# Hybrid mLSTM and HGRN2 decoder layer on one core: denominators summed on VectorE, the last norm's sums in halves and its variance earlier

## The chip, the cores and the metric

One core of a Trainium2 chip. The metric is device time in microseconds of one launch. The weights come from HBM, everything else stays on the chip between the stages except for some intermediate tiles that are spilled to HBM and loaded back. Engines: TensorE (PE, with its weight loads as PEld), VectorE (DVE), ScalarE (ACT), GpSimd (POOL) and SyncE (SP), which issues nearly all DMAs; POOL issues eight near the end.

## The reference

One step of a decoder layer for 256 prompt tokens and 64 sample tokens (8 sequences of 8), 320 tokens in all, all in 4-byte floats. Cut to what the change touches:

```python
# mLSTM, per head (4 heads, DK 256, DV 512), chunkwise
s   = einsum('bhtk,bhsk->bhts', qc, kc) * d
num = einsum('bhts,bhsv->bhtv', s, vc) + w_inter * einsum('bhtk,bhkv->bhtv', qc, C)
den = sum(s, axis=-1) + w_inter * einsum('bhtk,bhk->bht', qc, n)
h   = num / maximum(abs(den), exp(-m_t))
# layer
x1  = LayerNorm(alpha * x + mix, ln1_g, ln1_b)
hid = square(relu(x1 @ w_up))
y   = LayerNorm(alpha * x1 + hid @ w_down, ln2_g, ln2_b)
```

Beside y the outputs are the final mLSTM and HGRN2 states of both groups (for the prompt: Cp, 4 heads of 256 x 512, and Sp, 8 heads of 128 x 256).

## The kernel before

Activations lie transposed, a tile being 128 features by 320 tokens. All dense layers are one stream of 304 weight tiles of 2048 x 128, in the order of a table: the gates and the input projections of the mLSTM heads (stage up to 400 us), those of the HGRN2 heads, the two branch projections, the output projection, and four groups of 16 up and 16 down tiles. A 4-byte product is made of fast products on halves: a number is split into a high half (a copy on ScalarE, `ACT wh`, or `bb`) and a low half (a subtraction on VectorE, line 491), and three products xh.wh, xl.wh and xh.wl are added in PSUM. A tile is two units of 1024 rows; a unit is 8 x 3 = 24 products. A unit's weights land in one of three raw buffers (`wr`) and are split into a pair of buffers from the list `hl_free`: three pairs `wh`, `wl` from the start, and five wide ones in `bb` in the late stages, of which one (`wx[4]`) holds halves for the first norm and is then given back to the list.

Beside this stream run chains: small generators of the form "acquire a buffer, wait for an event, issue one instruction on this engine". A planner written in Python (`Sched`) keeps a clock for each engine, and after each triple of wide products lets every chain issue what its clock says is ready. The order that results is fixed in the program; on the chip each engine takes its own list in order and waits on semaphores. `Pool` objects hand out buffers, PSUM banks among them (`mbank`, `sbank`).

The change touches these chains:

- `m_S` (one per mLSTM head) makes the gated score blocks in E: columns 0 to 127 for the first half of the prompt against itself, 128 to 255 and 256 to 383 for the second half against both halves, 384 to 511 (partitions 64 to 127) for the sample.
- `m_num` makes the numerators of the prompt and its denominators, as products of a block of E with a column of ones: one for the first half, two that are added in PSUM for the second.
- `m_sample` does the same for the sample: one product for the block of E, two for the halves of `qn`, which holds query times normaliser.
- `m_C` and `h_S` make the prompt's final states behind the last weights, with operands that were spilled to HBM and come back by POOL's DMAs into buffers that the weights leave free. `m_C` makes two products of six parts per head into `oC`, `h_S` one per head into `oS`.
- `ln_add`, `ln_sum`, `ln_pre`, `ln_final`, `ln_scale` are the two norms. The sums S1 (of z) and S2 (of z squared) are added up over tiles on VectorE, and the sum over partitions is a product with a matrix of ones: in `total` on halves, elsewhere on 4-byte numbers. After four tiles a first mean `cb` is taken out of z. Tile 15 is not added but goes into PSUM by products of its own (`ln_final`), on top of `ln_pre`. `ln_scale` makes mean M, variance X and the reciprocal root RS.
- `y` subtracts the mean from the 16 tiles of z (line 1960), multiplies by the root (line 1965); `yb_` applies scale and shift on ScalarE and stores two tiles by one DMA.

Of the kernel before, what the change touches and what calls it, by code (L numbers as in the profile page):

```python
# [256 lines left out]
def post(ev):  # L257
    return ("set", ev)
# [51 lines left out]
class Program:  # L310
# [48 lines left out]
    def carve(self):  # L359
# [30 lines left out]
        self.qz = Pool([self.qz0])  # L390
        self.tst = Pool([B(320) for _ in range(2)])
        self.tst2 = B(320)
# [24 lines left out]
        self.sg = Pool([Part(self.f2, 4912)(320), self.tst2])  # L417
        B = Part(self.f2, 4304)
        self.sr = Pool([B(320) for _ in range(2)])
# [493 lines left out]
    def m_S(self, h):  # L913
# [22 lines left out]
        yield ("dve", dve(128), lambda: v.tensor_tensor(ss[64:128, 128:256], E[64:128, 384:512], f(ss[64:128, 0:128]), ALU.subtract))  # L936
        yield ("act", act(256), lambda: self.A(ss[0:64], f(ss[64:128])))
        yield post(m["S"])

# [119 lines left out]
    def m_num(self, h):  # L1059
# [12 lines left out]
        yield ("pe", 212, lambda: self.mm(db[:, 0:1], E[:, 0:128], one, start=True, stop=True))  # L1072
        yield ("pe", 212, lambda: self.mm(db[:, 1:2], E[:, 128:256], one, start=True, stop=False))
        yield ("pe", 212, lambda: self.mm(db[:, 1:2], E[:, 256:384], one, start=False, stop=True))
        for i in range(2):
# [29 lines left out]
    def m_C(self, h):  # L1105
        k = yield acq(self.kx)
        kt = yield ("pool", 1000, lambda: self.nc.gpsimd.dma_start(
            k.rearrange("p x s k -> p (x s k)").rearrange("p (y k) -> p y k", k=128), self.kD[h].rearrange("y p k -> p y k")))
        w = yield acq(self.vx)
        vt = yield ("pool", 1000, lambda: self.nc.gpsimd.dma_start(w, self.vD[h]))  # L1110
        e = Ev()
        e.t = max(kt, vt) + 4000.0
        yield wait(e, self.main_end)
        for c in range(2):
            if h:
                yield wait(self.ln[1]["fin"])
            b = yield acq(self.mbank)
            yield ("pe", 6 * pe_r(512), lambda: [self.mm(
                b, k.rearrange("p x s k -> p (x s k)")[:, 512 * x + 256 * c + 128 * s:512 * x + 256 * c + 128 * s + 128], w[:, y, s, :], start=n == 0, stop=n == 5)
                for n, (s, x, y) in enumerate((s, x, y) for s in range(2) for x, y in ((0, 0), (0, 1), (1, 0)))])  # L1120
            if c == 1:
                yield post(self.mh[h]["C"])
            if h < 2 and c == 0:
                yield ("dve", dve(512, True), lambda: self.nc.vector.tensor_copy(self.oC[h][:, c, :], b))
            else:
                yield ("act", act(512, True), lambda: self.A(self.oC[h][:, c, :], b))
            yield rel(self.mbank, b)
            yield ("sp", 620, lambda: self.dma(self.d["Cp"][h, :, c, :], self.oC[h][:, c, :]))
        yield rel(self.vx, w)

    def place(self, to, x):
# [13 lines left out]
    def m_sample(self, h):  # L1145
# [8 lines left out]
        for c in range(2):  # L1154
            qc = cap(qz, 256 * c, [[136, 2], [32, 4], [1, 8]])
            yield ("dve", dve(64), lambda: v.tensor_tensor(qc, by_token(qk[:, c, :], 256, False), by_token(bc, 640, False), ALU.mult))
            n4 = cap(self.n0[:, h, c, :], 0, [[4, 2], [1, 4], [0, 8]])
            yield ("dve", dve(64), lambda: v.tensor_tensor(by_token(qn, 128 * c, True), qc, n4, ALU.mult))
        yield post(m["QW"])
        nb = yield acq(self.sbank)  # L1160
# [420 lines left out]
    def h_S(self, h):  # L1581
# [7 lines left out]
        yield ("pe", 2 * pe_f(256), lambda: [self.mm(  # L1589
            b[:, 0:256], x[:, 128 * i:128 * i + 128], x[:, 256 + 256 * i:512 + 256 * i], start=i == 0, stop=i == 1) for i in range(2)])  # L1590
        if h < 4:
            yield ("act", act(256, True), lambda: self.A(self.oS[:, h, :], b[:, 0:256]))
# [151 lines left out]
    def ln_add(self, n, j, z, pre):  # L1744
# [4 lines left out]
        if j < 4:  # L1749
# [39 lines left out]

    def total(self, p, x, hl):  # L1790
        hi, lo = hl[:, 0, :], hl[:, 1, :]
        yield from self.split(x, hi, lo)
        for i, y in enumerate((hi, lo)):
            yield ("pe", 147, lambda: self.mm(p[:, :TOK], self.ones.bitcast(F32R), y, start=i == 0, stop=i == 1))

# [33 lines left out]
    def ln_scale(self, n):  # L1829
# [9 lines left out]
        for p in st["p"]:  # L1839
            yield rel(self.sbank, p)  # L1840
        yield ("dve", dve(TOK, mode=2), lambda: v.tensor_scalar(X, X, 0.0, EPS, ALU.max, ALU.add))
        yield ("act", act(TOK), lambda: self.A(RS, X, AF.Ln))
        yield ("act", act(TOK), lambda: self.A(RS, RS, AF.Exp, scale=-0.5))
# [108 lines left out]
    def y(self):  # L1952
# [3 lines left out]
        yield wait(st["m"])  # L1956
        for i in range(KT + 6):
            if i < KT:
                z = self.acc[:, i, :]
                yield ("dve", dve(TOK), lambda: v.tensor_tensor(z, z, self.lnb[3], ALU.subtract), (0.0,))  # L1960
            if i == 5:
                yield wait(st["end"])
            if i > 5:
                z = self.acc[:, i - 6, :]
                t = yield ("dve", dve(TOK), lambda: v.tensor_tensor(z, z, self.lnb[4], ALU.mult), (0.0,))
                self.s.spawn(self.yb_(i - 6, z), 0, t)

# [8 lines left out]
    def run(self, pool):  # L1976
# [12 lines left out]
        self.vD = [self.dr.tile([128, 2, 2, 512], F32, name=f"vD{j}") for j in range(MH)]  # L1989
        self.ln = [dict(c=Ev(), end=Ev(), pre=Ev(), m=Ev(), fin=Ev(), s=[Ev() for _ in range(KT)]) for _ in range(2)]  # L1990
        self.xq, self.xq_ev = [None] * KT, [Ev() for _ in range(KT)]
# [82 lines left out]
```

## Time and profile before

| | |
|---|---|
| three runs | 2311.4, 2311.3, 2310.22 us, median 2311.3 |
| profiled execution | 2310.56 us, of which 2308.7 us span |
| granted TensorE clock | 0.999 |
| HBM traffic | 183 GB/s over the span |
| first state product behind the stream starts | 2281.72 us |
| last state product ends | 2300.8 us |

Times inside the span count from its first instruction. In the timeline a row is: start, duration, engine, line, operation, output tile <- input tiles, shapes, count, and in brackets the idle time before it and who ended it. Line 346 is the helper of every ScalarE operation and line 352 that of every product, so tiles tell them apart: `misc` is the column of ones, `ones` the matrix of ones, `f` a work area of VectorE, `f3m` the tiles of z, `vec` scale and shift, `oC` and `oS` the final states. A 4-byte product shows as two records (x2).

### The profile page before, as it was taken

The numbers are of one execution on the slowest core, as the hardware profiler recorded it, in microseconds if no ns is written. First come the engines' busy times: TensorE is split into PE (matmuls) and PEld (weight loads), VectorE is DVE, ScalarE is ACT, GpSimd is POOL, SyncE is SP. The second block draws the span as 40 slices with busy tenths as digits, with TensorE's granted clock in tenths as the row PEclk, the third lists the DMA queues.
The fourth block names the chain that finished last, engine by engine and source line by source line (L and its number), as shares of the span: only waits on it lengthen the run. The fifth ranks groups of instructions, "written<-read, shape, count | busy, mean of one in ns | idle before, by whom it ended". The sixth has DMA issues, their size and how long they took to land.

```text
span 2308.7 us, 38882 instructions
## 1 busy us (share of the span) xinstructions
PE 2299.2 (100%) x15712; PEld 2258.4 (98%) x15712; DVE 1365.3 (59%) x2333; ACT 1040.1 (45%) x1664; POOL 13.3 (1%) x37
## 2 busy tenths in 40 slices
PE   9999999999999999999999999999999999999998
PEld 9999999999999999999999999999999999999997
DVE  6566667666767776555555767654444444444455
ACT  5443444555556565444433446533433343234333
POOL 0000000000000000000000000000000000000000
PEclk9999999999999999999999999999999999999999
DMA  7677797666556565555555654444444444444466
GB/s 282 209 248 250 236 292 240 204 189 187 183 182 200 170 191 171 176 172 177 170 175 174 213 165 156 146 147 149 152 148 154 146 152 150 148 154 146 154 214 190
DMA packets 214573, 424.94 MB, mean 184 GB/s; under 512 B 83572, under 2 KB 110068, under 8 KB 213368
## 3 DMA queue, kind: packets, MB, share of 16 engines
q1 hardware_dynamic: 209512, 415.97, 55.7%
q0 software_dynamic: 4736, 6.29, 1.1%
q8 instruction: 123, 2.02, 0.4%
q14 instruction: 58, 0.48, 0.1%
q10 hardware_dynamic: 144, 0.20, 0.0%
HBM read 371.48 MB, written 50.90 MB: 183 GB/s over the span
## 4 chain that ended last, share of the span: by engine, by line
PE 99%; ACT 1%; DVE 0%; issue 0%; ACTq 0%; POOL 0%; DVEq 0%; POOLq 0%
PE bank L352 98%; ACT f3m L346 0%; PE bank L954 0%; PE bank L1465 0%; DVE f3m L1960 0%; ACT f L346 0%; PE bank L1470 0%; PE bank L1519 0%; PE bank L1022 0%; PE bank L1626 0%; PE bank L1191 0%; ACT oC L346 0%; ACT oS L346 0%; ACT bb L346 0%; ACT xh L346 0%
## 5 line engine op out<-in xcount | busy, mean ns | idle before, releaser
L352 PE MATMUL bank<-xh,wh 128*128 128x320 f32 (+1 forms) x2432 | 781.3, 322 | 0.0
L352 PE MATMUL bank<-xh,wl 128*128 128x320 f32 (+1 forms) x2432 | 752.2, 310 | 0.0
L352 PE MATMUL bank<-xl,wh 128*128 128x320 f32 (+1 forms) x2432 | 750.0, 309 | 0.0
L491 DVE TENSOR_TENSOR wl<-wr,wh 128x1024 fp32r<-128x1024 f32 x426 | 522.1, 1226 | 381.4 <-ACT wh L346 378.5
L346 ACT ACTIVATE wh<-wr 128x1024 fp32r<-128x1024 f32 x426 | 450.9, 1059 | 514.9 <-PE bank L352 498.1
L352 PEld LDWEIGHTS bank<-xh,wh 128*128 128x128 f32 x2432 | 458.1, 189 | 18.0 <-issue 15.5
L352 PEld LDWEIGHTS bank<-xl,wh 128*128 128x128 f32 x2432 | 458.4, 189 | 3.3
L352 PEld LDWEIGHTS bank<-xh,wl 128*128 128x128 f32 x2432 | 458.0, 188 | 0.2 <-DVE wl L491 0.2
L491 DVE TENSOR_TENSOR bb<-wr,bb 128x1024 fp32r<-128x1024 f32 x176 | 215.7, 1225 | 227.6 <-ACT bb L346 227.5
L346 ACT ACTIVATE bb<-wr 128x1024 fp32r<-128x1024 f32 x176 | 186.4, 1059 | 311.4 <-PE bank L352 293.9
L352 PE MATMUL bank<-xh,bb 128*128 128x320 f32 (+1 forms) x1280 | 285.4, 309 | 0.0
L352 PE MATMUL bank<-rxb,bb 128*128 128x320 f32 x1208 | 276.3, 309 | 0.0
L352 PE MATMUL bank<-ra,wh 128*128 128x320 f32 x988 | 265.9, 309 | 0.0
L352 PE MATMUL bank<-ra,bb 128*128 128x320 f32 x1096 | 264.3, 309 | 0.7 <-DVE ra L1657 0.7
L352 PEld LDWEIGHTS bank<-xh,bb 128*128 128x128 f32 x1280 | 215.0, 188 | 0.0
L352 PEld LDWEIGHTS bank<-rxb,bb 128*128 128x128 f32 x1208 | 204.2, 188 | 0.2
L352 PE MATMUL bank<-xl,bb 128*128 128x320 f32 (+1 forms) x640 | 197.7, 309 | 0.0
L352 PEld LDWEIGHTS bank<-ra,bb 128*128 128x128 f32 x1096 | 187.1, 188 | 1.2 <-DVE ra L1657 0.9
L352 PEld LDWEIGHTS bank<-ra,wh 128*128 128x128 f32 x988 | 176.3, 188 | 0.0
L352 PE MATMUL bank<-rxb,wh 128*128 128x320 f32 x548 | 169.0, 308 | 0.0
L352 PE MATMUL bank<-rxb,wl 128*128 128x320 f32 x548 | 169.0, 308 | 0.0
L352 PEld LDWEIGHTS bank<-xl,bb 128*128 128x128 f32 x640 | 120.4, 188 | 0.2 <-DVE xl L1885 0.2
(262 smaller groups left out, 2195.3 us busy)
## 6 DMA issues: line engine op xcount, KB each, us to landing
wr<-wt SPq DMA_DIRECT2D x602, 512.0 KB, 3.4
rx<-C SPq DMA_DIRECT2D x34, 256.0 KB, 4.8
Cs<-rx SPq DMA_DIRECT2D x34, 256.0 KB, 5.3
f<-C SPq DMA_DIRECT2D x30, 256.0 KB, 5.2
Cs<-f SPq DMA_DIRECT2D x30, 256.0 KB, 5.0
f<-first SPq DMA_DIRECT2D x6, 704.0 KB, 10.3
vD<-ra SPq DMA_DIRECT2D x4, 1024.0 KB, 5.6
f<-S SPq DMA_DIRECT2D x8, 512.0 KB, 6.3
```

The costliest lines, as they stand in the source:

```text
L346: return self.nc.scalar.activation(out, in_, func, **kw)
L352: self.nc.tensor.matmul(*a, **kw)
L491: self.V().tensor_tensor(lo, raw, hi.bitcast(F32), ALU.subtract)
```

## The change

Denominators: in `m_S` VectorE adds the second half's two blocks, and `m_num` has one product for them; in `m_sample` VectorE adds the two halves of `qn`, and later the block of E onto it, and one product is left. Last norm: its three sums over partitions that were products on 4-byte numbers (`ones` with S1 after four tiles, S1 and S2 in `ln_pre`) are made by `total` on halves, as in the first norm; the halves lie in `wx[4]`, which is therefore no longer given back. In `y` one subtraction instead of six is issued ahead of the variance, two more wait for it, and the others alternate with the multiplications. The evictions of `m_C` and `h_S` become chains of their own, all of `m_C`'s on ScalarE, and all but the first product of `m_C` wait until the last norm's sums are issued. Two work areas move by 128 columns.

```diff
@@ m_S
         yield ("act", act(256), lambda: self.A(ss[0:64], f(ss[64:128])))
+        yield ("dve", dve(128), lambda: v.tensor_tensor(E[:, 256:384], E[:, 256:384], E[:, 128:256], ALU.add))
         yield post(m["S"])
@@ m_num
-        yield ("pe", 212, lambda: self.mm(db[:, 1:2], E[:, 128:256], one, start=True, stop=False))
-        yield ("pe", 212, lambda: self.mm(db[:, 1:2], E[:, 256:384], one, start=False, stop=True))
+        yield ("pe", 212, lambda: self.mm(db[:, 1:2], E[:, 256:384], one, start=True, stop=True))
@@ m_C
-            if h:
+            if h or c:
                 yield wait(self.ln[1]["fin"])
...
-            if h < 2 and c == 0:
-                yield ("dve", dve(512, True), lambda: self.nc.vector.tensor_copy(self.oC[h][:, c, :], b))
-            else:
-                yield ("act", act(512, True), lambda: self.A(self.oC[h][:, c, :], b))
...
+            self.s.spawn(self.C_out(h, c, b), 0, self.s.t["pe"])
@@ m_sample
+        yield ("dve", dve(128), lambda: v.tensor_tensor(qn[:, 0:128], qn[:, 0:128], qn[:, 128:256], ALU.add))
         yield post(m["QW"])
...
+        yield ("dve", dve(128), lambda: v.tensor_tensor(qn[64:128, 0:128], qn[64:128, 0:128], E[64:128, 384:512], ALU.add))
         db = yield acq(self.sbank)
-        yield ("pe", 212, lambda: self.mm(db[:, 0:1], E[:, 384:512], self.one, start=True, stop=False))
-        for c in range(2):
-            yield ("pe", 212, lambda: self.mm(db[:, 0:1], qn[:, 128 * c:128 * c + 128], self.one, start=False, stop=c == 1))
+        yield ("pe", 212, lambda: self.mm(db[:, 0:1], qn[:, 0:128], self.one, start=True, stop=True))
@@ ln_add
-                if n == 0:
-                    yield from self.total(p, S1, self.lns[0])
-                else:
-                    yield ("pe", pe_f(TOK), lambda: self.mm(p[:, :TOK], self.ones, S1, start=True, stop=True))
+                yield from self.total(p, S1, self.lns[0])
...
-            self.hl_free.append((self.s.t["pe"], self.wx[4]))
@@ ln_pre
-            yield ("pe", pe_f(TOK), lambda: self.mm(p[i][:, :TOK], self.ones, self.lnb[i], start=True, stop=False))
+            yield from self.total(p[i], self.lnb[i], self.lns[1 + i], False)
@@ ln_scale
         yield ("dve", dve(TOK, mode=2), lambda: v.tensor_scalar(X, X, 0.0, EPS, ALU.max, ALU.add))
+        if n:
+            yield post(st["x"])
@@ y
-        for i in range(KT + 6):
+        for i in range(KT + 3):
...
-            if i == 5:
+            if i == 0:
+                yield wait(st["x"])
+            elif i == 2:
                 yield wait(st["end"])
-            if i > 5:
+            if i > 2:
```

Three places show how the planner's order moves. First TensorE, at the last sample denominators of the first mLSTM head, where `misc` is the column of ones, `f_76` the area of E and `qn`, `ra` the operands of other small products, and `xh`, `wh` the wide stream. Before:

```order
L352 MATMUL bank_85<-misc,f_76 128x1
L352 MATMUL bank_82<-xh,wh 128x320
L352 MATMUL bank_82<-xl,wh 128x320
L352 MATMUL bank_82<-xh,wl 128x320
L352 MATMUL bank_88<-ra 128x512
L352 MATMUL bank_82<-xh,wh 128x320
L352 MATMUL bank_82<-xl,wh 128x320
L352 MATMUL bank_82<-xh,wl 128x320
L352 MATMUL bank_85<-misc,f_76 128x1
```

Now, the same place:

```order
L352 MATMUL bank_88<-ra 128x512
L352 MATMUL bank_85<-misc,f_76 128x1
L352 MATMUL bank_82<-xh,wh 128x320
L352 MATMUL bank_82<-xl,wh 128x320
L352 MATMUL bank_82<-xh,wl 128x320
L352 MATMUL bank_88<-ra 128x512
```

One denominator product is left of three, and it stands right behind another small product, with no wide one between.

Second VectorE, from the eviction of the last tile (bank_81) on; line 1960 (now 1963) subtracts the mean, 1838 (now 1839) makes the variance, 1844 to 1846 (now 1847 to 1849) the root, 1965 (now 1970) multiplies. Before:

```order
L1940 TENSOR_TENSOR f3m<-f3m,bank_81 128x320
L1124 COPY oC<-bank_85 128x512
L1960 TENSOR_TENSOR f3m<-f3m,f_76 128x320 x6
L1838 SCALAR_TENSOR_TENSOR f_76<-bank_84,f_76 128x320
L1841 TENSOR_SCALAR f_76<-f_76 128x320
L1844 SCALAR_TENSOR_TENSOR f_76<-f_76 128x320
L1124 COPY oC<-bank_88 128x512
L1845 TENSOR_TENSOR f_76<-f_76 128x320
L1846 SCALAR_TENSOR_TENSOR f_76<-f_76 128x320
L1960 TENSOR_TENSOR f3m<-f3m,f_76 128x320
L1965 TENSOR_TENSOR f3m<-f3m,f_76 128x320
```

Now:

```order
L1943 TENSOR_TENSOR f3m<-f3m,bank_81 128x320
L1963 TENSOR_TENSOR f3m<-f3m,f_76 128x320
L1839 SCALAR_TENSOR_TENSOR f_76<-bank_84,f_76 128x320
L1842 TENSOR_SCALAR f_76<-f_76 128x320
L1963 TENSOR_TENSOR f3m<-f3m,f_76 128x320 x2
L1847 SCALAR_TENSOR_TENSOR f_76<-f_76 128x320
L1848 TENSOR_TENSOR f_76<-f_76 128x320
L1849 SCALAR_TENSOR_TENSOR f_76<-f_76 128x320
L1963 TENSOR_TENSOR f3m<-f3m,f_76 128x320
L1970 TENSOR_TENSOR f3m<-f3m,f_76 128x320
```

The variance moves ahead of all but one subtraction, and both copies of state blocks are gone from VectorE.

Third ScalarE, from the eviction of the mean and its square on (`f_76<-bank_87`, now `f_76<-bank_86`; `f_76<-f_76` are logarithm and exponential of the root; `f3m<-f3m,vec` is scale and shift of a tile of y). Before:

```order
L346 ACTIVATE f_76<-bank_87 128x320 x2
L346 ACTIVATE oC<-bank_86 128x512
L346 ACTIVATE f_76<-f_76 128x320 x2
L346 ACTIVATE oC<-bank_82 128x512
L346 ACTIVATE oC<-bank_83 128x512
L346 ACTIVATE f3m<-f3m,vec 128x320 x2
L346 ACTIVATE oC<-bank_81 128x512
L346 ACTIVATE f3m<-f3m,vec 128x320 x2
L346 ACTIVATE oC<-bank_85 128x512
L346 ACTIVATE f3m<-f3m,vec 128x320 x2
L346 ACTIVATE oC<-bank_86 128x512
```

Now:

```order
L346 ACTIVATE oC<-bank_87 128x512
L346 ACTIVATE f_76<-bank_86 128x320 x2
L346 ACTIVATE f_76<-f_76 128x320
L346 ACTIVATE oC<-bank_85 128x512
L346 ACTIVATE f_76<-f_76 128x320
L346 ACTIVATE oC<-bank_88 128x512
L346 ACTIVATE oC<-bank_82 128x512
L346 ACTIVATE f3m<-f3m,vec 128x320
L346 ACTIVATE oC<-bank_81 128x512
L346 ACTIVATE f3m<-f3m,vec 128x320 x2
L346 ACTIVATE oC<-bank_87 128x512
L346 ACTIVATE f3m<-f3m,vec 128x320 x2
```

The eviction of the first state product now stands ahead of the mean, that of the second has moved from ahead of the logarithm to between it and the exponential, and one scaled tile, no longer two, stands ahead of the next eviction.

More of the change, by code (lines that the diff above doesn't have):

```diff
@@ L390, in carve @@
         self.qz = Pool([self.qz0])
-        self.tst = Pool([B(320) for _ in range(2)])
+        self.tst = Pool([B(256) for _ in range(2)])
         self.tst2 = B(320)
@@ L417, in carve @@
         self.sg = Pool([Part(self.f2, 4912)(320), self.tst2])
-        B = Part(self.f2, 4304)
+        B = Part(self.f2, 4176)
         self.sr = Pool([B(320) for _ in range(2)])
@@ L1122, in m_C, with C_out @@
                 yield post(self.mh[h]["C"])
-            if h < 2 and c == 0:
-                yield ("dve", dve(512, True), lambda: self.nc.vector.tensor_copy(self.oC[h][:, c, :], b))
-            else:
-                yield ("act", act(512, True), lambda: self.A(self.oC[h][:, c, :], b))
-            yield rel(self.mbank, b)
-            yield ("sp", 620, lambda: self.dma(self.d["Cp"][h, :, c, :], self.oC[h][:, c, :]))
+            self.s.spawn(self.C_out(h, c, b), 0, self.s.t["pe"])
         yield rel(self.vx, w)
+    def C_out(self, h, c, b):
+        yield ("act", act(512, True), lambda: self.A(self.oC[h][:, c, :], b))
+        yield rel(self.mbank, b)
+        yield ("sp", 620, lambda: self.dma(self.d["Cp"][h, :, c, :], self.oC[h][:, c, :]))
     def place(self, to, x):
@@ L1590, in h_S, with S_out @@
             b[:, 0:256], x[:, 128 * i:128 * i + 128], x[:, 256 + 256 * i:512 + 256 * i], start=i == 0, stop=i == 1) for i in range(2)])
+        self.s.spawn(self.S_out(h, b), 0, self.s.t["pe"])
+    def S_out(self, h, b):
         if h < 4:
@@ L1788, in ln_add, with total @@
             self.s.spawn(self.ln_pre(n), 0)
-    def total(self, p, x, hl):
+    def total(self, p, x, hl, stop=True):
         hi, lo = hl[:, 0, :], hl[:, 1, :]
@@ L1793, in total @@
         for i, y in enumerate((hi, lo)):
-            yield ("pe", 147, lambda: self.mm(p[:, :TOK], self.ones.bitcast(F32R), y, start=i == 0, stop=i == 1))
+            yield ("pe", 147, lambda: self.mm(p[:, :TOK], self.ones.bitcast(F32R), y, start=i == 0, stop=stop and i == 1))
     def ln_sum(self, j, z):
@@ L1960, in y @@
                 yield ("dve", dve(TOK), lambda: v.tensor_tensor(z, z, self.lnb[3], ALU.subtract), (0.0,))
-            if i == 5:
+            if i == 0:
+                yield wait(st["x"])
+            elif i == 2:
                 yield wait(st["end"])
-            if i > 5:
-                z = self.acc[:, i - 6, :]
+            if i > 2:
+                z = self.acc[:, i - 3, :]
                 t = yield ("dve", dve(TOK), lambda: v.tensor_tensor(z, z, self.lnb[4], ALU.mult), (0.0,))
-                self.s.spawn(self.yb_(i - 6, z), 0, t)
+                self.s.spawn(self.yb_(i - 3, z), 0, t)
     def yb_(self, j, z):
@@ L1989, in run @@
         self.vD = [self.dr.tile([128, 2, 2, 512], F32, name=f"vD{j}") for j in range(MH)]
-        self.ln = [dict(c=Ev(), end=Ev(), pre=Ev(), m=Ev(), fin=Ev(), s=[Ev() for _ in range(KT)]) for _ in range(2)]
+        self.ln = [dict(c=Ev(), end=Ev(), pre=Ev(), m=Ev(), fin=Ev(), x=Ev(), s=[Ev() for _ in range(KT)]) for _ in range(2)]
         self.xq, self.xq_ev = [None] * KT, [Ev() for _ in range(KT)]
```

## The prediction

> **What bounds the kernel now.** I read the page first, then the table of waits of TensorE, then windows, then the timeline at the places that the change touches.
>
> From the page, busy time by engine and the granted clock in 40 slices:
>
> ```profile
> PE 2299.2 (100%) x15712; PEld 2258.4 (98%) x15712; DVE 1365.3 (59%) x2333; ACT 1040.1 (45%) x1664; POOL 13.3 (1%) x37
> PEclk9999999999999999999999999999999999999999
> ```
>
> The waits of TensorE over the whole span (waited for: total us, times, longest):
>
> ```profile
> PE bank L352 <- POOL ones L634: 1.0, 1, 1.0
> PE bank L352 <- DVE ra L1657: 0.7, 1, 0.7
> ```
>
> TensorE runs without a gap at full clock; 1.7 us is all that it waits for another engine. Up to its last product the time is the sum of what is issued to it, so a product taken out there is worth its full price, and work added on VectorE (59%) or ScalarE (45%) is worth nothing unless TensorE comes to wait for it. Only the end differs. Windows there (span, then busy time of PE, PEld, DVE, ACT, POOL; last clock, DMA share, GB/s):
>
> ```profile
> 2292.00:2296.00 4.00, 4.00 (x20) 3.43 (x19) 4.00 (x11) 3.85 (x8) 0.00 (x0) 1.00 0.70 266
> 2296.00:2300.00 4.00, 4.00 (x20) 3.52 (x19) 4.00 (x11) 4.00 (x10) 0.00 (x0) 1.00 0.80 298
> 2300.00:2304.00 4.00, 0.82 (x4) 0.38 (x2) 2.41 (x7) 3.18 (x7) 0.00 (x0) 0.94 1.01 365
> ```
>
> From 2292 us VectorE and ScalarE are full, from 2300 the DMA engines are, and TensorE is finished at 2300.8. The end hangs on the last norm and its stores.
>
> **Part 1: twelve denominator products fewer.** Each head of the mLSTM had six products of one column (three in the token part, three in the sample part) and has three now: 12 fewer. The price is read from the starts of TensorE's instructions around one:
>
> ```profile
> 99.92 0.31 PE L352 MATMUL bank<-xh,wl 128*128 128x320 f32 x1
> 100.07 0.28 PE L352 MATMUL bank<-misc,f 128*128 128x1 f32 x2
> 100.21 0.39 PE L352 MATMUL bank<-xh,wh 128*128 128x320 f32 x1
> 100.44 0.31 PE L352 MATMUL bank<-xl,wh 128*128 128x320 f32 x1
> ```
>
> Wide products follow one another at 0.147 us (99.92 to 100.07). From 99.92 to 100.44 there would be two such steps, 0.29; there are 0.52. One denominator product costs 0.23 us: 0.14 for itself and 0.09 in the step of the wide product behind it. 12 x 0.23 = 2.8 us. This is on the path, since TensorE is.
>
> The Trainium skill (TensorE: Matmul & The Clock Gate, section Back-to-back issue gap) gives about 60 cycles, an issue floor of 25 ns, for a product of 1 to 64 columns; for the two records of one denominator that would be 50 ns, an estimate from that page, 12 of them 0.6 us and not 2.8. The trace disagrees with 0.23 us each, and I go by the trace.
>
> In return come 12 additions on VectorE, the nearest row being an addition of the same size:
>
> ```profile
> L982 DVE TENSOR_TENSOR f<-f 128x128 fp32r<-128x128 f32 x8 | 2.3, 287 | 0.8 <-ACT f L346 0.8
> L491 DVE TENSOR_TENSOR wl<-wr,wh 128x1024 fp32r<-128x1024 f32 x426 | 522.1, 1226 | 381.4 <-ACT wh L346 378.5
> ```
>
> 12 x 0.29 = 3.5 us, in the stage up to 400 us, where the idle of VectorE covers it. If the cover fails, a denominator product waits in TensorE's queue with the wide products behind it; that is the slow rival below.
>
> **Part 2: the sums of the last norm in halves.** Three 4-byte sums over all partitions (one behind tile 3 of the last group, two in the last tile) become pairs of products on a high and a low half. A sum as it is now, and one of those that the first norm already makes in halves:
>
> ```profile
> 2276.09 0.31 PE L352 MATMUL bank<-rxb,bb 128*128 128x320 f32 x1
> 2276.24 0.70 PE L352 MATMUL bank<-f,ones 128*128 128x320 f32 x2
> 2276.53 0.55 PE L352 MATMUL bank<-rxb,bb 128*128 128x320 f32 x1
> 2276.92 0.31 PE L352 MATMUL bank<-ra,bb 128*128 128x320 f32 x1
> ...
> 1296.12 0.31 PE L352 MATMUL bank<-rxb,wl 128*128 128x320 f32 x1
> 1296.27 0.30 PE L352 MATMUL bank<-bb,ones 128*128 128x320 f32 x1
> 1296.41 0.31 PE L352 MATMUL bank<-rxb,wh 128*128 128x320 f32 x1
> ```
>
> 2276.09 to 2276.92 is 0.83, less two steps of 0.147 is 0.54 us for a full sum. A product on a half takes one ordinary step (1296.27 to 1296.41), two of them 0.29. Saved: 3 x 0.25 = 0.7 us. Each sum now needs a copy on ScalarE and a subtraction on VectorE ahead of it. For the two in the last tile these lie here:
>
> ```profile
> 2274.88 0.49 DVE L1806 TENSOR_TENSOR f<-f 128x320 f32<-128x320 f32 x1
> 2281.72 1.55 PE L352 MATMUL bank<-bb,wh 128*128 128x512 f32 x6
> ```
>
> The running sums are complete at 2275.4; four steps of about 0.5 end at 2277.4, and the last tile lasts until 2281.7. The cover is 4 us. The price of the halves is one pair of weight buffers: the first norm used it and gave it back, and now it is kept, so seven pairs instead of eight hold prepared weights during the last 256 units. A unit is 24 products, 3.5 us, so the lead falls from 28 to 25 us; a unit needs its load (median 3.4 us), 1.06 on ScalarE and 1.23 on VectorE. I count nothing.
>
> **Part 3: order.** By the new order five fewer runs of small products interrupt the wide ones than the removals alone would give, since some now stand side by side. At 0.09 us a return to wide products that is at most 0.45 us; I take 0.3, bounds 0 and 0.5. The stream comes to 2.8 + 0.7 + 0.3 = 3.8 us.
>
> **Part 4: the end.** Before, as the timeline has it:
>
> ```profile
> 2283.84 0.77 ACT L346 ACTIVATE f<-bank 128x320 f32<-128x320 f32 x2 [0.87 <-PE bank L352]
> 2284.31 2.50 DVE L1960 TENSOR_TENSOR f3m<-f3m,f 128x320 f32<-128x320 f32 x6 [0.32 <-ACT f L346]
> 2286.73 0.48 DVE L1838 SCALAR_TENSOR_TENSOR f<-bank,f 128x320 f32<-128x320 f32 x1
> 2287.61 0.98 ACT L346 ACTIVATE f<-f 128x320 f32<-128x320 f32 x2 [1.24 <-DVE f L1841]
> 2288.62 0.49 DVE L1844 SCALAR_TENSOR_TENSOR f<-f 128x320 f32<-128x320 f32 x1 [1.04 <-ACT f L346]
> 2289.03 0.68 DVE L1124 COPY oC<-bank 128x512 f32<-128x512 f32 x1
> 2290.95 0.48 DVE L1965 TENSOR_TENSOR f3m<-f3m,f 128x320 f32<-128x320 f32 x1
> 2291.47 1.46 ACT L346 ACTIVATE f3m<-f3m,vec 128x320 f32<-128x320 f32 x2 [1.01 <-DVE f3m L1965]
> 2300.35 2.83 ACT L346 ACTIVATE f3m<-f3m,vec 128x320 f32<-128x320 f32 x5
> 2303.90 1.05 SPq L355 DMA_DIRECT2D Sp<-oS  x2
> ```
>
> The mean and its square leave ScalarE at 2284.6, but the variance (L1838) begins at 2286.7, behind six subtractions. With one ahead it begins at about 2284.8: 1.9 us gained. The copy of a state block in the middle of the root (2289.03, about 0.5 on VectorE's queue) goes to ScalarE, where one such eviction now stands between logarithm and exponential, about 0.5: even. Another stands ahead of the mean, in ScalarE's idle 0.87 us of the first row. The two subtractions let through behind the variance lie beside ScalarE's two functions. So the first scaled tile starts at about 2289.5 on this clock instead of 2291.47: 1.9 to 2.0.
>
> From there ScalarE is the bound. Its chain shows the price of each kind:
>
> ```profile
> 2294.54 0.48 ACT oC L346
> 2295.02 1.12 ACT f3m L346 x2
> 2297.75 0.55 ACT oS L346 x2
> ```
>
> Before: 16 x 0.56 + 3 x 0.48 + 4 x 0.275 = 11.5 us, from 2291.5 to 2303.0, and the row of five ends at 2303.18. After: four state evictions instead of three stand behind the first scaled tile, so 12.0 us, from 2289.5 to 2301.6. The last store of y then goes 1.5 us earlier, and the stores of Sp behind it in SP's queue with it. The DMA engines, full from 2300, get the same bytes sooner and had room before (0.70, 0.80). I take 1.5 us, bounds 0 (if the stores do not move) and 2.2.
>
> **Sum.** 2.8 + 0.7 + 0.3 + 1.5 = 5.3 us. The profiled run took 2310.56 us, of which 2308.7 are the span; that makes 2305.3. The three runs have a median of 2311.3, 0.7 higher, which is the clock on which I give the time: 2311.3 - 5.3 = 2306.0 us, 0.23% less.
>
> **The rivals.**
>
> *The end gives nothing (2307.5).* The state products of the fourth head need a 1 MB load into the buffer that the last weight unit leaves free. That unit was the one before the last, and by the new order it is the last one, so this load starts some 3.9 us later.
>
> ```profile
> 2278.12 0.55 POOL L1110 DMA_DIRECT2D bb<-vD  x1 [5.40 <-PE bank L352]
> bb<-vD POOLq DMA_DIRECT2D x1, 1024.0 KB, 7.2
> bb<-vD POOLq DMA_DIRECT2D x1, 1024.0 KB, 8.2
> 2291.03 1.52 PE L352 MATMUL bank<-bb,wh 128*128 128x512 f32 x6
> ```
>
> The issue moves to about 2282.0, the landing with 7.2 to 8.2 us to 2289.2 to 2290.2. The fourth head now comes seventh of the eight state products, at 2291.0 in this timeline: 0.8 us to spare at the worst, and as much again before ScalarE, which reaches that eviction at 2293.4, would stand. At 10.5 us the gain of the end begins to shrink, at 12 it is gone: 2311.3 - 3.8 = 2307.5. The Trainium skill (DMA: Bandwidth & Descriptors, section Anatomy of one DMA, SWDGE path) has 2.0 us and the bytes at 436 GB/s, 4.4 us for this load, an estimate by which the rival could not be; the trace has 7.2 and 8.2, so it stays. Full DMA engines to the very end would have the same effect.
>
> *VectorE's queue holds the denominators up (2323).* Eight products now wait for an addition; in three heads the sample addition stands right behind a weight split of 1.23 us, which itself waits for ScalarE. A split is idle 381.4 / 426 = 0.90 us on the mean before it starts. If each of the eight products waits for both, 8 x 2.13 = 17.0 us come back: 2306.0 + 17.0 = 2323.0. The sign turns at 0.66 us a wait, and from 1.24 it is over 0.2% slower. Against it: products wait for VectorE's results throughout the span, and it cost 0.7 us once.
>
> *The removed products were nearly free (2308.2).* This is what the issue floor would give: 12 x 0.05 = 0.6 in place of 2.8. Then 2311.3 - 3.1 = 2308.2. The gaps of the trace speak against it.
>
> **How the numbers follow.** A difference under 0.2% (4.6 us, the line at 2306.7) is about what a measurement of this kernel can't tell from no change. The forecast has 0.70: within it the regrouping and the end reach from 2305.1 (0.5 and 2.2 us) to 2307.3 (0 and 0.5 us), and about four fifths lie below 2306.7, 0.56. The end without gain has 0.19, the nearly free products 0.03, both within 0.2%. The waits on VectorE have 0.08, three quarters of it slower by more than 0.2%. Faster 0.56, same 0.38, slower 0.06. The range takes in the best bounds with 0.4 us for the scatter of runs (2304.7) and both cases within 0.2% (2308.4), and leaves out the waits.
>
> **What would show it.** Right: 12 fewer one-column products (24 records instead of 48), TensorE's waits unchanged, the last wide product 3.5 to 4 us earlier, the variance within 0.6 us of the square, ScalarE's last scaled tile about 5 us earlier than 2303.2. Wrong: a new wait of TensorE on an addition, on the 1 MB load at the seventh state product, or a last store that has not moved against the last wide product.

## The result and the profile after

The changed kernel takes 2304.93 us (median of 12 runs, 2304.25 to 2307.19) against 2311.01 us for the kernel before (12 runs, 2309.24 to 2311.41). The ratio is 0.9976, 95% interval 0.9968 to 0.9984: 6.1 us or 0.24% faster; the forecast's line of 0.2% lies inside the interval. The forecast was 2306.0 us, range 2304.7 to 2308.4. The profiled execution took 2304.6 us, its span 2302.8; before it was 2310.56 and 2308.7, so the spans differ by 5.9 us, and that is the difference which is taken apart here.

Busy time by engine, from the page of the changed kernel:

```profile
PE 2295.4 (100%) x15688; PEld 2254.7 (98%) x15688; DVE 1370.2 (59%) x2346; ACT 1043.0 (45%) x1669; POOL 13.3 (1%) x37
```

TensorE has 24 records fewer and is busy 3.8 us less; VectorE has 13 instructions more. TensorE's waits (waited for: total us, times, longest):

```profile
PE bank L352 <- POOL ones L634: 1.0, 1, 1.0
PE bank L352 <- DVE ra L1662: 0.7, 1, 0.7
```

They are the two of before, with the same lengths: no wait on an addition. Groups of TensorE by form, changed kernel (count, then busy us and mean ns):

```profile
L352 PE MATMUL bank<-bb,ones 128*128 128x320 f32 x12 | 3.7, 307 | 0.0
L352 PE MATMUL bank<-misc,f 128*128 128x1 f32 x24 | 3.3, 208 | 0.0
L352 PE MATMUL bank<-f,ones 128*128 128x320 f32 x2 | 0.7, 432 | 0.0
```

24 records of one column instead of 48, six products on halves more, six records of 4-byte sums fewer. Then the end, from the timeline of the changed kernel (start, us, engine, line):

```profile
2277.98 1.54 PE L352 MATMUL bank<-bb,wh 128*128 128x512 f32 x6
2280.10 0.77 ACT L346 ACTIVATE f<-bank 128x320 f32<-128x320 f32 x2
2280.98 0.48 DVE L1839 SCALAR_TENSOR_TENSOR f<-bank,f 128x320 f32<-128x320 f32 x1
2285.59 0.66 ACT L346 ACTIVATE f3m<-f3m,vec 128x320 f32<-128x320 f32 x1 [0.23 <-DVE f3m L1970]
2295.53 2.29 ACT L346 ACTIVATE f3m<-f3m,vec 128x320 f32<-128x320 f32 x4
2296.76 1.42 SPq L355 DMA_DIRECT2D y<-f3m  x3
2298.27 0.95 SPq L355 DMA_DIRECT2D Sp<-oS  x2
```

The first product of the state (bb,wh) stands right behind the last tile in both kernels, so it divides the stream from the end. It starts at 2277.98 instead of 2281.72: the stream gave 3.74 us. From that start on the two kernels stand thus, each figure a difference of rows shown here or in the prediction:

| us behind the first state product | before | after |
|---|---|---|
| variance starts (L1838, now L1839) | 5.01 | 3.00 |
| first scaled tile starts | 9.75 | 7.61 |
| last scaled tile ends | 21.46 | 19.84 |
| last issue of Sp ends | 23.23 | 21.24 |
| span ends | 26.98 | 24.82 |

The end gave 2.16 us, and 3.74 + 2.16 = 5.9.

### The profile page after: what moved, and what is told of

Read it like the earlier page. It is cut to its first block, busy times and chain, and to the rows that moved or that the text cites. A ratio compares the mean times of both kernels' runs of the same rounds, so it can differ in the third digit from the quotient of the medians.

```text
span 2302.8 us, 38823 instructions
## 1 busy us (share of the span) xinstructions
PE 2295.4 (100%) x15688; PEld 2254.7 (98%) x15688; DVE 1370.2 (59%) x2346; ACT 1043.0 (45%) x1669; POOL 13.3 (1%) x37
## 4 chain that ended last, share of the span: by engine, by line
PE 99%; DVE 0%; ACT 0%; issue 0%; ACTq 0%; POOL 0%; DVEq 0%; POOLq 0%
PE bank L352 98%; PE bank L955 0%; DVE f3m L1963 0%; DVE f3m L1970 0%; PE bank L1466 0%; ACT f3m L346 0%; PE bank L1471 0%; PE bank L1520 0%; PE bank L1023 0%; PE bank L1631 0%; PE bank L1192 0%; ACT f L346 0%; ACT oS L346 0%; ACT oC L346 0%; ACT wh L346 0%
## 5 line engine op out<-in xcount | busy, mean ns | idle before, releaser
L352 PE MATMUL bank<-xh,wh 128*128 128x320 f32 (+1 forms) x2504 | 802.2, 321 | 0.0
L352 PE MATMUL bank<-xh,wl 128*128 128x320 f32 (+1 forms) x2504 | 774.8, 310 | 0.0
L352 PE MATMUL bank<-xl,wh 128*128 128x320 f32 (+1 forms) x2504 | 771.8, 309 | 0.0
L352 PE MATMUL bank<-xh,bb 128*128 128x320 f32 (+1 forms) x1136 | 253.9, 309 | 0.0
L352 PE MATMUL bank<-rxb,bb 128*128 128x320 f32 x1088 | 249.0, 309 | 0.0
L352 PEld LDWEIGHTS bank<-xh,bb 128*128 128x128 f32 x1136 | 191.0, 188 | 0.0
L352 PE MATMUL bank<-rxb,wl 128*128 128x320 f32 x608 | 187.6, 308 | 0.0
L352 PEld LDWEIGHTS bank<-rxb,bb 128*128 128x128 f32 x1088 | 184.3, 187 | 0.0
L352 PE MATMUL bank<-xl,bb 128*128 128x320 f32 (+1 forms) x568 | 175.5, 309 | 0.0
L352 PE MATMUL bank<-bb,wh 128*128 128x320 f32 (+1 forms) x536 | 119.0, 313 | 0.0
## 6 DMA issues: line engine op xcount, KB each, us to landing
f<-first SPq DMA_DIRECT2D x6, 704.0 KB, 10.6
```

The lines of the kernel that those rows point to most:

```text
L352: self.nc.tensor.matmul(*a, **kw)
```

## The experiments

The theory was the prediction's: TensorE's stream is worth its removed products at full price, and the end is worth what ScalarE's chain gains. The rivals were that the removed products were nearly free, that VectorE would hold products up, and that a load or the full DMA engines would eat the gain of the end. First each part alone, put into the kernel before (each with the two moves of work areas).

**One product a denominator, the rest as before.**

```diff
@@ m_S
+        yield ("dve", dve(128), lambda: v.tensor_tensor(E[:, 256:384], E[:, 256:384], E[:, 128:256], ALU.add))
@@ m_num
-        yield ("pe", 212, lambda: self.mm(db[:, 1:2], E[:, 128:256], one, start=True, stop=False))
-        yield ("pe", 212, lambda: self.mm(db[:, 1:2], E[:, 256:384], one, start=False, stop=True))
+        yield ("pe", 212, lambda: self.mm(db[:, 1:2], E[:, 256:384], one, start=True, stop=True))
...
```

and in m_sample the two additions and the one product of the change.

> Before with the denominators of the change alone (12 one-column products fewer, 12 additions on VectorE). The sum of the prediction: 12 x 0.23 = 2.8 us off the stream, so the first state product starts at about 2278.9 us in the trace instead of 2281.7, the end behind it is as long as before (27.0 us), and the time is 2308.2. If a removed product cost only the issue floor: 0.6 us, start at 2281.1, time 2310.4. If TensorE waits for the additions: new waits of TensorE for VectorE of over 0.66 us each and a time above 2311.

2308.85 us against 2311.07 (ratio 0.9991, interval 0.9982 to 1.0): 2.2 us less. The end behind the first state product is as long as before (26.9 us). In the trace the first state product starts at 2279.96, only 1.76 earlier, and there is a wait of TensorE on a load of the old state. The groups that multiply by the old state, of before, and then of this kernel:

```profile
L352 PE MATMUL bank<-rx,f 128*32 128x512 f32 x68 | 11.2, 598 | 0.0
L352 PE MATMUL bank<-f 128*32 128x512 f32 x60 | 10.4, 599 | 0.0
```

```profile
L352 PE MATMUL bank<-rx,f 128*32 128x512 f32 x68 | 11.6, 599 | 0.0
L352 PE MATMUL bank<-f 128*32 128x512 f32 x60 | 11.0, 599 | 0.5 <-DMA f<-C 0.5
```

They are busy for 22.6 us instead of 21.6. Counted by starts (from each product's start to the next start on TensorE) they take 17.03 us instead of 15.55, so 1.5 us of the gain is lost there. By the same count the one-column records and the wide products behind them take 2.7 us less, which is the price of the prediction; the remaining 0.5 us of the 1.76 is spread thinly over the other products. The same two groups are busy for 21.5 us in the changed kernel and between 20.9 and 22.6 in the other traces (but for the one with added products). Most of these differences go with the loads of the old state: TensorE's weight loads wait for them for 0.8 us before, 0.6 in the changed kernel and 1.7 here, so one execution waits for these loads more than another.

**The sums of the last norm in halves, the rest as before.**

```diff
@@ ln_add
-                    yield ("pe", pe_f(TOK), lambda: self.mm(p[:, :TOK], self.ones, S1, start=True, stop=True))
+                yield from self.total(p, S1, self.lns[0])
...
-            self.hl_free.append((self.s.t["pe"], self.wx[4]))
@@ ln_pre
-            yield ("pe", pe_f(TOK), lambda: self.mm(p[i][:, :TOK], self.ones, self.lnb[i], start=True, stop=False))
+            yield from self.total(p[i], self.lnb[i], self.lns[1 + i], False)
```

> Before with the three sums of the last norm in halves alone, the fifth wide buffer pair kept for them. The sum of the prediction: 3 x 0.25 = 0.7 us off the stream (first state product at about 2281.0), end unchanged, time 2310.3; no wait of TensorE beyond the 1.7 us of before. If the missing buffer pair matters, TensorE waits for weights in the up and down stages and the time is above 2311.

2310.92 us (0.9999, 0.999 to 1.0008): too little to be told from nothing. Its trace does not begin the state products earlier but 0.35 us later, at 2282.07:

```profile
2282.07 1.54 PE L352 MATMUL bank<-bb,wh 128*128 128x512 f32 x6
```

In this execution the products on the old state were busy for 11.9 + 10.7 = 22.6 us, 1.0 more than before (by starts 16.5 us, also 1.0 more). The starts around the sums give their price without that. Before, a sum cost 0.54 us (its two records and what the wide product behind them took over its usual step); here two products on halves step 0.147 us each and the wide product behind them steps 0.146, as usual, which makes 0.29. The three sums are 0.73 us cheaper, where 0.7 was forecast. TensorE's waits are those of before, so the copies and subtractions in front are covered.

**The variance ahead of all but one subtraction, the rest as before.**

```diff
+        if n:
+            yield post(st["x"])
...
-        for i in range(KT + 6):
+        for i in range(KT + 3):
...
-            if i == 5:
+            if i == 0:
+                yield wait(st["x"])
+            elif i == 2:
                 yield wait(st["end"])
-            if i > 5:
+            if i > 2:
...
```

> Before with the order of the last norm alone (one subtraction ahead of the variance, two behind it). The stream is unchanged: first state product at 2281.7. If the variance was what held the end, the first scaled tile comes 1.9 us sooner after the first state product than the 9.75 us of before, and the time falls by 1.5 to 2.2 us, to about 2309.2. If the stores are what binds, the first scaled tile comes sooner and the last transfer does not: 2311.0.

2309.7 us (0.9994, 0.9985 to 1.0003), 1.4 less. The timeline of this kernel, with the first state product at 2281.56:

```profile
2284.56 0.48 DVE L1838 SCALAR_TENSOR_TENSOR f<-bank,f 128x320 f32<-128x320 f32 x1
2287.20 0.68 DVE L1124 COPY oC<-bank 128x512 f32<-128x512 f32 x1
2289.12 0.48 DVE L1969 TENSOR_TENSOR f3m<-f3m,f 128x320 f32<-128x320 f32 x1
2289.71 0.60 ACT L346 ACTIVATE oC<-bank 128x512 f32<-128x512 f32 x1 [0.76 <-PE bank L352]
2290.20 1.19 ACT L346 ACTIVATE f3m<-f3m,vec 128x320 f32<-128x320 f32 x2
2298.14 3.43 ACT L346 ACTIVATE f3m<-f3m,vec 128x320 f32<-128x320 f32 x6
```

The variance gains the full 2.0 us, but the copy of a state block is still in the middle of the root, and on ScalarE an eviction stands in front of the first scaled tile: that starts 8.64 us behind the state product, 1.1 earlier than before and 1.0 later than in the changed kernel. At the last scaled tile (2298.14 + 3.43) little of that 1.0 is left: it ends 20.01 us behind the state product, 1.45 earlier than before and only 0.17 later than in the changed kernel, because here three state evictions stand behind the first scaled tile and there four.

**The state evictions on ScalarE, the rest as before.**

```diff
@@ m_C
-            if h:
+            if h or c:
...
-            if h < 2 and c == 0:
-                yield ("dve", dve(512, True), lambda: self.nc.vector.tensor_copy(self.oC[h][:, c, :], b))
...
+            self.s.spawn(self.C_out(h, c, b), 0, self.s.t["pe"])
...
+        self.s.spawn(self.S_out(h, b), 0, self.s.t["pe"])
```

> Before with the evictions of the state products alone as chains of their own, all eight of the mLSTM on ScalarE. The stream is unchanged. By the prediction VectorE is freed of a copy in the middle of the root (0.5 us) and ScalarE gets 0.5 us more in the same place: 0, within 0.3 us, time 2311.0. If these copies are what held the end, most of the 2.2 us that the end gained are here: 2309.

2311.14 us (1.0001, 0.9992 to 1.001): nothing. The variance still stands behind six subtractions (2286.85, 5.01 behind the state product at 2281.84), and the first scaled tile starts 9.62 us behind that product. Alone the evictions are worth 0.1 us there. At the last scaled tile they cost something:

```profile
2302.49 1.20 ACT L346 ACTIVATE f3m<-f3m,vec 128x320 f32<-128x320 f32 x2
```

It ends 21.85 us behind the state product, 0.39 later than before, with four state evictions instead of three behind the first scaled tile; and TensorE waits 0.5 us for an eviction of `oS` ahead of its last products.

The four medians add to 3.7 us (2.2 + 0.15 + 1.4 - 0.07), not 6.1, and each part's interval reaches to no change. Either the scatter of the executions hides the rest or the parts need each other; so the stream and the end were run as halves, beside the changed kernel.

**The variance and the evictions together:** the two diffs above in one kernel.

> The variance ahead of all but one subtraction together with the state evictions on ScalarE; denominators and sums as before. If the two need each other (the copy taken out of the root shortens it by 0.5 us, and the fifth eviction no longer stands in front of the first scaled tile), the end behind the first state product is 24.8 to 25.0 us instead of 27.0, the first scaled tile comes 7.6 us behind that product instead of 9.7, and the time is 2.1 us below the kernel before, 2309.0. If they simply add as they measured alone (1.3 us shorter and 0.1 longer), the end is 25.7 us and the time 2309.8. The stream up to the state products is unchanged but for waits on loads of the old state.

2309.35 us against 2311.07 (0.9993, 0.9985 to 1.0002): 1.7 less, between the two cases. The chain does what the first case said, the span does not:

```profile
2281.89 1.55 PE L352 MATMUL bank<-bb,wh 128*128 128x512 f32 x6
2289.50 0.66 ACT L346 ACTIVATE f3m<-f3m,vec 128x320 f32<-128x320 f32 x1 [0.22 <-DVE f3m L1974]
2299.44 2.29 ACT L346 ACTIVATE f3m<-f3m,vec 128x320 f32<-128x320 f32 x4
2300.66 1.76 SPq L355 DMA_DIRECT2D y<-f3m  x3
2302.51 0.96 SPq L355 DMA_DIRECT2D Sp<-oS  x2
```

First scaled tile at 7.61 us and last one done at 19.84 behind the state product, to the hundredth as in the changed kernel: on the engines the two edits together are worth 2.14 and 1.62 us at these two places, where the variance alone gained 1.11 and 1.45 and the evictions alone gained 0.13 and lost 0.39. Behind that the last issues took 0.34 us longer and what comes behind them 0.75, and the span of 2307.8 ends 25.9 us behind the state product, not 24.8. In this trace the end is thus no shorter than with the variance alone (25.6). Why the stores took longer in this execution is open.

**The denominators and the halves together:** their two diffs in one kernel.

> The denominators and the sums in halves together; the last norm's order and the evictions as before. If the prices of the trace hold (24 records of 0.070 us, 14 returns to wide products at 0.08, three sums at 0.24), the time is 1.7 + 1.1 + 0.7 = 3.5 us below the kernel before, 2307.6. If the two changes cost each other something, as their medians apart suggest (2.2 and 0.1), it is 2308.7. The end behind the first state product stays at 27.0 us.

2308.04 us (0.9987, 0.9979 to 0.9996): 3.0 less, between the two cases. The state products start at 2278.82, 2.9 earlier, and the products on the old state were busy for 11.5 + 10.6 = 22.1 us, 0.5 more than before (by starts also 0.5 more). The end behind the first state product is 26.9 us. One row shows a rival at work:

```profile
2285.76 3.00 PE L352 MATMUL bank<-bb,wl 128*128 128x512 f32 x12 [0.20 <-DMA bb<-vD]
```

With the sums in halves the 1 MB load of the fourth head goes out one unit later, and here, where that head comes fifth, TensorE waits 0.2 us for it: the load lands 6.5 us behind its issue at 2279.13, at 2285.6. With the halves alone, in the same order, it took 5.5 us, and TensorE did not wait.

**The changed kernel once more.**

> The changed kernel once more, in the same call as its two halves. If the halves add, it lies below the kernel before by their sum, some 5.6 us; its executions differ by up to 2 us by what TensorE waits for the loads of the old state (its products on them took 15.4 us in the first trace of it, 17.0 and 16.5 in two of the parts), and the median lies between 2304.9 and 2305.8.

2305.61 us (0.9977, 0.9968 to 0.9986), 5.5 less. The two halves give 1.7 + 3.0 = 4.7; the 0.7 that is missing lies within the intervals, each of which is about 2 us to either side. Its trace repeats the first one: state products at 2277.84, first scaled tile at 2285.46 and span 2302.6, 7.62 and 24.8 us behind them.

**Each denominator product of the changed kernel made five times.** 48 products more; the result is that of the last one.

```diff
@@ m_num
+        for _ in range(5):
+            yield ("pe", 212, lambda: self.mm(db[:, 0:1], E[:, 0:128], one, start=True, stop=True))
+            yield ("pe", 212, lambda: self.mm(db[:, 1:2], E[:, 256:384], one, start=True, stop=True))
@@ m_sample
+        for _ in range(5):
+            yield ("pe", 212, lambda: self.mm(db[:, 0:1], qn[:, 0:128], self.one, start=True, stop=True))
```

> The changed kernel with each of its 12 denominator products made five times (48 more one-column products, same result). By the gaps of the trace 0.14 us of a product is its own and 0.09 the return to the wide stream, so 48 more cost 6.7 us if they all stand side by side and 11.0 if each stands alone: 2311.6 to 2316. By the issue floor of 25 ns a record they cost 48 x 0.05 = 2.4: 2307.3.

2326.45 us (1.0063 of the kernel before, 1.0046 to 1.008), 21.5 over the changed kernel, twice the upper bound of what was expected. The price of a product holds; one of the added ones, and the group:

```profile
114.38 0.28 PE L352 MATMUL bank<-misc,f 128*128 128x1 f32 x2
114.52 0.39 PE L352 MATMUL bank<-xh,wh 128*128 128x320 f32 x1
114.75 0.31 PE L352 MATMUL bank<-xl,wh 128*128 128x320 f32 x1
```

```profile
L352 PE MATMUL bank<-misc,f 128*128 128x1 f32 x120 | 16.6, 209 | 0.0
```

114.38 to 114.75 is 0.37, less one step of 0.147 is 0.22 us. Counted over all starts, the 96 records more stand for 6.8 us. 46 more wide products stand behind a denominator, but fewer behind other small products, so the longer steps of the wide products cost 1.2 us more in all: 8.1 us, inside 6.7 to 11.0. Of the other 13 us, these waits hold 5.6:

```profile
PE bank L955 <- DVE f L1253: 3.4, 1, 3.4
PE bank L352 <- DVE f L1253: 1.2, 1, 1.2
PE bank L1023 <- DVE f L983: 1.0, 1, 1.0
```

TensorE stands for VectorE's update of the state (L1253) and for its split of the values (L983). That the longer groups of small products push the heads back to there is the likely reason and is not shown; the rest is spread over the starts of the other small products, and was not followed further. VectorE's queue can thus hold TensorE up, at five times the products and not at a fifth of them, but none of these rows is a wait on one of the additions that the rival named.

**The changed kernel without seven of the eight stores of Cp** (those blocks of the output stay unwritten), to see whether the full DMA engines set the end.

```diff
+        if h == 3 and c == 1:
+            yield ("sp", 620, lambda: self.dma(self.d["Cp"][h, :, c, :], self.oC[h][:, c, :]))
```

> The changed kernel without seven of the eight 256 KB stores of Cp (1.8 MB less to write; only the last block is stored). All of them are issued before the last 8 us. If the DMA engines, full from 2290 us in the trace of the changed kernel, set the end, the last transfer lands about 1 us sooner after its issue and the time falls by 1 to 1.5 us, to about 2303.7. If ScalarE's last tiles and SP's queue set it, the end does not move by more than 0.4 us: 2304.9, less the SP time of three stores that stand between those of y (about 0.1 us).

2305.76 us, no faster than the changed kernel. Its state products start 1.3 us later (2279.28), behind a wait of 0.7 us on a load of the old state. Windows at its end (span, busy time of PE, PEld, DVE, ACT, POOL; clock, DMA share, GB/s):

```profile
2288.00:2292.00 4.00, 4.00 (x20) 3.34 (x19) 4.00 (x11) 4.00 (x9) 0.00 (x0) 1.00 0.42 164
2292.00:2296.00 4.00, 4.00 (x20) 3.54 (x19) 4.00 (x11) 3.85 (x9) 0.00 (x0) 1.00 0.69 265
```

and the same stretch of the changed kernel:

```profile
2288.00:2292.00 4.00, 4.00 (x20) 3.41 (x19) 4.00 (x11) 4.00 (x8) 0.00 (x0) 1.00 0.98 372
2292.00:2296.00 4.00, 4.00 (x20) 3.54 (x19) 4.00 (x11) 3.85 (x10) 0.00 (x0) 1.00 0.90 336
```

The DMA engines drop from 0.98 and 0.90 to 0.42 and 0.69. Part of this drop is the later start: in windows moved by 1.3 us, which hold the same work, the shares are 0.59 and 0.85. Yet with the engines that much emptier in the first of them, the span of 2304.0 ends 24.7 us behind the first state product, as it does with the stores. So the bytes of Cp do not set the end; what is left for it is the chain on VectorE and ScalarE and the last stores behind it. In the four microseconds after these windows the engines are full without the Cp stores too:

```profile
2296.00:2300.00 4.00, 2.38 (x12) 1.74 (x10) 3.04 (x9) 3.12 (x7) 0.00 (x0) 1.00 1.00 362
```

so whether the last stores of y and Sp are themselves held up by full engines is not answered by this run.

## Why the prediction was right, step by step

**Part 1, 2.8 us: held, as 2.7.** The denominators alone took 2.2 us off the median, which by itself is not clear of the scatter. The starts settle it. Over the whole stream the one-column records take 3.38 us before and 1.66 in the changed kernel, 1.7 less; and 24 wide products stand behind a denominator before and 12 now, each of them stepping 0.231 us where a wide one behind a wide one steps 0.147: 12 x 0.084 = 1.0. 1.7 + 1.0 = 2.7, in the trace of the denominators alone as well. The rival of nearly free products falls with this and with the fivefold run, since each product has 0.22 to 0.23 us by its starts. The floor of 25 ns that the Trainium skill gives (TensorE: Matmul & The Clock Gate, section Back-to-back issue gap) would make 12 x 0.05 = 0.6 us of it, an estimate from that page; the traces disagree.

**Part 2, 0.7 us: held in the trace, not to be seen in the time.** The steps give 0.73; the median of the part alone moved by 0.15 us, inside its interval.

**Part 3, 0.3 us: not there.** Five returns to wide products fewer were expected from the regrouping, at 0.09 us each. Beside the twelve of Part 1 four are gone, with the denominators alone as well. But they stood behind fast products (the kind that is used on halves) of 320 to 512 columns, and a wide product behind one of those takes an ordinary step. One such place before:

```profile
102.29 0.40 PE L352 MATMUL bank<-ra 128*128 128x512 f32 x1
102.52 0.31 PE L352 MATMUL bank<-xh,wh 128*128 128x320 f32 x1
102.67 0.30 PE L352 MATMUL bank<-xl,wh 128*128 128x320 f32 x1
```

102.52 to 102.67 is 0.15. What this part had wrong is that it gave every return the price that the rows show behind a denominator, a 4-byte product. With 2.7, 0.7 and the 0.1 that the products on the old state took less in this execution, 3.5 of the 3.74 us are accounted for; the rest is spread over the steps of other products. That 3.74 came so close to the forecast's 3.8 is in part luck: in the three other traces with both changes of the stream the first state product starts 3.9, 2.9 and 2.4 us earlier than before, mostly by what the products on the old state took (14.8, 16.1 and 17.2 us by starts, 15.4 in the changed kernel's first trace).

**Part 4, 1.5 us with bounds 0 and 2.2: the mechanism right, the size at the upper bound.** The variance started 2.0 us earlier against the state product (1.9 forecast), the first scaled tile 2.14 (1.9 to 2.0 forecast), the last scaled tile ended 1.62 earlier (1.5). What was not foreseen lies behind it: before, the span ended 5.52 us behind the last scaled tile, now 4.98, and 4.9 in the two other traces with this end (the changed kernel once more, and without the Cp stores). Of these 0.54 us, 0.37 lie between the last scaled tile and the end of the last issue in SP's queue, 0.17 behind that. In the trace of variance and evictions alone the same stretch took 6.1, so the gain behind the chain is not settled by the edits alone, and that the end came out at 2.16 and not at the 1.6 of the chain is not explained. The end as a whole repeats: it is 26.9 us in the three traces that change the stream alone, and 24.7 to 24.8 in the three of the changed kernel, with and without the stores of Cp.

One sentence of this part was wrong without effect: "From there ScalarE is the bound." The chain of waits of the changed kernel (start, us, what), around the first scaled tile and where VectorE hands over:

```profile
2284.75 0.40 DVE f3m L1963
2285.15 0.40 DVE f3m L1970
2285.55 0.40 DVE f3m L1963
...
2292.39 0.41 DVE f3m L1970
2292.80 0.02 issue
2292.83 0.65 ACT f3m L346
2293.48 0.54 ACT oS L346 x2
2294.02 1.08 ACT f3m L346 x2
2295.11 0.55 ACT oS L346 x2
```

Until 2292.8 it is VectorE, subtracting and multiplying in turn at 0.40 us each, since three more of the subtractions now stand between the products; only then is ScalarE the bound. The two engines need nearly the same time for two tiles and an eviction (four VectorE steps of 0.40, 1.60; 2293.48 to 2295.11 on ScalarE, 1.63), so that the sum came out is a coincidence of these two sizes.

**The rivals.** The 1 MB load did come close. Its issue and landing in the changed kernel, the fifth state product, and the seventh (with the eighth), which needs it:

```profile
2278.30 0.55 POOL L1110 DMA_DIRECT2D bb<-vD  x1 [5.29 <-PE bank L352]
bb<-vD POOLq DMA_DIRECT2D x1, 1024.0 KB, 8.4
2284.57 1.52 PE L352 MATMUL bank<-bb,wl 128*128 128x512 f32 x6
2287.29 2.88 PE L352 MATMUL bank<-bb,wl 128*128 128x512 f32 x12
```

2278.30 + 8.4 = 2286.7, 0.6 us ahead of its product; the working had 0.8 at the worst. That the new order puts this head seventh is what keeps it hidden: the fifth product starts at 2284.57, so with this head there TensorE would have stood for some 2.1 us, an estimate from these rows. In the run with the denominators, the halves and the old order of the end, where it did come fifth, TensorE waited 0.2 us for a load of 6.5. The Trainium skill's line (DMA: Bandwidth & Descriptors, section Anatomy of one DMA, SWDGE path) makes 4.4 us of this load, an estimate by which there would have been no risk; this trace has 8.4. The hold-up by VectorE did not come: TensorE's waits are unchanged.

## What to carry to other kernels

A short product between wide ones is to be priced by the starts around it, its own step and the longer step of the wide product behind it, and where TensorE has no gaps that price is paid in full. The longer step is not paid behind every small product, so look at what stands in front before counting returns. Two edits at the end of a kernel can need each other at one place and hardly at the next: at the first scaled tile the early variance alone gained 1.1 us and ran into the copy in the root, and with the evictions moved it gained 2.1; at the last scaled tile it was 1.45 alone and 1.6 with them. In the medians (1.4 alone, 1.7 together) the difference is not to be told from the scatter. And before medians of single parts are added, look in the trace for what differs from one execution to the next; here it is as large as the parts.

## What was not expected of the hardware

The step of a wide product depends on the kind of product in front of it. Behind a 4-byte product of at most 128 columns on the whole array it is 0.23 us on the mean, behind one of 256 columns 0.34, and behind a 4-byte sum of 320 columns 0.39 (2276.53 to 2276.92 in the rows of the prediction); behind a fast product on the whole array, of 256 to 512 columns, it is the usual 0.146 to 0.148. These are the starts of the trace of before. Loads that land just in time go with the scatter of one and the same program: the products on the old state were busy for 20.9 us in one execution of the changed kernel and 21.5 in another, and for 22.6 in two of the kernels with parts of it. And 48 added products worth 8.1 us cost 21.5; of the rest 5.6 us are waits on VectorE, and where the others come from is open.
